# First-norm scales on TensorE, gate rows in twos, and a ScalarE copy ahead of the weights' sums in a one-layer encoder kernel

## The chip, the cores and the metric

The kernel runs on one core of a Trainium2 chip. The metric is the device time of one execution in microseconds (us); "the time" below is the median of the runs shown. The core has five engines with a queue each: TensorE (PE in the profile; its weight loads are the row PEld), VectorE (DVE), ScalarE (ACT), GpSimd (POOL) and SyncE (SP), whose queue issues the DMAs here. An engine takes its queue in order, and an instruction that waits holds up those behind it.

## The reference, cut to what matters

One transformer-like layer runs over 64 + 512 = 576 tokens of two request groups (`c_sample`, `c_prompt`), with model width 1024:

```python
mod = jax.nn.silu(c) @ w_ada + b_ada          # one row for each group
sh1, sc1, gt1, sh2, sc2, gt2 = split(mod, 6)
h = rmsnorm(x, norm1_g) * (1 + sc1) + sh1
proj = h @ w_in                               # q, k, v, GLU, two gates
m = (sigmoid(g_a) * attention @ w_attn_out + sigmoid(g_b) * conv_branch) @ w_out
x = x + gt1 * m
h2 = rmsnorm(x, norm2_g) * (1 + sc2) + sh2
gate, up = split(h2 @ w_ffn_up, 2)
x = x + gt2 * ((silu(gate) * up) @ w_ffn_down)
y = rmsnorm(x, final_g)
```

All inputs and outputs are float32.

## The kernel before, in words

The model's 1024 columns lie on the partitions as 8 tiles of 128; the 576 tokens run along the free dimension, in two halves. Every float32 weight and activation is split into a high part, rounded to the type that TensorE reads in one pass (fp32r), and a low part, the rest; a product is then three passes (`mm3`, L323 to L325). Weights come by DMA from SyncE's queue into a ring of five raw buffers (`wraw`, `load_raw`, L248). `split_unit` takes half a chunk, 128x512: ScalarE casts it to `whi` (L297), and POOL, or for some kinds VectorE, subtracts to get `wlo` (L300); each of these has four buffers. `weights` runs a few units ahead of the products.

Outside of blocks marked `manual_schedule` a planner sets the order on each engine from a simulation of times. In those blocks the order is that of the code, and the planner may put later work between.

**First norm and start of the input projection** (L501 to L582, ordered by hand). The conditioning vector is broadcast over the partitions (`cb`). For tile `k`, a scale needs a column of `w_ada`: two row products with a running sum on VectorE, one for each group (`ada_cols`, L416, tiles `dump`), called by `row`; then `scale` (L463) and `make_t` (L439) on VectorE, a high part on ScalarE (L475) and a low part on VectorE (L481), all in `make_h`. A shift is either made like that (`ROW_SH`: tiles 0 and 6) or by 8 products of 2 columns on TensorE (`ada_col`, L433), with the result in the PSUM tile `cols`. Meanwhile TensorE runs `kpass` (L498): for each tile `k` three passes (high x high, low weights x high, high weights x low of tile `k`), each over five chunks. `ada_col(k + 2)` stands ahead of the third pass of round `k`. After rounds 1 and 2, three and two split units are made.

**Up projection in pairs.** 22 pairs of a gate tile and an up tile are multiplied by a scheme of seven half-size products with sums of weights. `pair_source` makes these: for `m == 6` VectorE adds the two halves of the up chunk (L270, into a PSUM bank, `cva` or `sa` in turn) and subtracts a half of the gate chunk (L271); L274 (POOL) and L277 (VectorE) make two more sums. In `up`, VectorE's L1376, L1379, L1381, L1383 and L1387 combine product banks; ScalarE's L1373 and VectorE's L1374 make the high and low parts of the activation. Products come in three blocks of 8, 8 and 6 pairs (`FCH`), each followed by its share of the down projection (`down`, 8 output tiles, two halves each).

**Gate rows.** During the first block's down projection the last modulation (`gt2`) is made: `gate_start` loads the conditioning vectors into two `wraw` buffers and copies them into the banks `cva` and `sa`; `gate_row(n)`, once ahead of each output tile, loads one row of `w_ada` into a `wraw` buffer (L1245) and does the two row products and a bias (L1339) on VectorE.

Of the kernel before, what the change touches and what calls it, by code (L numbers as in the profile page):

```python
# [14 lines left out]
AF = mybir.ActivationFunctionType  # L15
# [4 lines left out]
P = 128  # L20
# [35 lines left out]

ROW_SH = (0, 6)

ROW_AT = 4
COL_SH = tuple(k for k in range(KT) if k not in ROW_SH)  # L60
# [27 lines left out]
def layer_kernel(ctx: ExitStack, tc: tile.TileContext, a):  # L88
# [96 lines left out]
    def vcol(o, i):  # L185
        return vec[:, o + i : o + i + 1]
# [67 lines left out]
    def pair_source(c, m):  # L254

        if m in (1, 2):
            return raws[c - 1][:, 4 * m - 4 : 4 * m]
        if m == 4:
            return raws[c][:, 4:8]
        g0, g1, u0, u1 = (raws[c - 1 + x // 2][:, 4 * (x % 2) : 4 * (x % 2) + 4] for x in range(4))  # L260
        if m == 6:

            n_sum[1] += 1
            if n_sum[1] == 1:
                sums[c, 5] = pair_sum()
                sums[c, 6] = bank("m0").rearrange("p (k n) -> p k n", n=P)
            else:
                two = bank2(("cva", "sa")[n_sum[1] % 2]).rearrange("p x (k n) -> p x k n", n=P)
                sums[c, 5], sums[c, 6] = two[:, 0], two[:, 1]
            nc.vector.tensor_add(out=sums[c, 5], in0=u0, in1=u1)  # L270
            nc.vector.tensor_sub(out=sums[c, 6], in0=sums[c, 5], in1=g0)  # L271
        elif m == 7:
            sums[c, 7] = pair_sum()
            nc.gpsimd.tensor_sub(out=sums[c, 7], in0=g0, in1=u0)  # L274
        elif m == 3:
            sums[c, 3] = pair_sum()
            nc.vector.tensor_sub(out=sums[c, 3], in0=g1, in1=sums[c, 6])  # L277
        return sums[c, m]
# [6 lines left out]

    def split_unit():
        i, key, k0, n, pair = units[state["unit"]]
# [10 lines left out]
        last = key[0] == "fd" and key[2] == len(FCH) - 1  # L298
        eng = nc.vector if last or (pair and pair[1] in LO_V) else nc.gpsimd
        eng.tensor_sub(out=lo, in0=src, in1=hi.bitcast(F32))  # L300
# [47 lines left out]
    with tc.tile_pool(name="sp", bufs=1) as sp:  # L348
# [6 lines left out]
        def load_wat(k):  # L355
# [3 lines left out]
            else:  # L359
                t = [sb([P, D], f"kv{2 * (k % 2)}"), sb([P, KT, P], f"kv{2 * (k % 2) + 1}")]  # L360
            nc.sync.dma_start(out=t[0], in_=a["w_ada_n"][k])
            if k in ROW_SH:
# [66 lines left out]
        def ada_col(k):  # L429
            if k in ROW_SH:  # L430
                return
            for i in range(KT):
                nc.tensor.matmul(  # L433
                    cols[:, 2 * k : 2 * k + 2], lhsT=wat[k][1][:, i], rhs=ct[:, i], start=i == 0, stop=i == KT - 1
                )

# [7 lines left out]
        def shift(k):  # L444
            f = SH1 + k
            src = cols[:, 2 * k : 2 * k + 2]
            if k in ROW_SH:
# [8 lines left out]
        def scale(k):  # L456
            if k == 0:
# [5 lines left out]
            nc.scalar.activation(  # L463
                out=sc_a[:, 0, k], in_=sc1[:, k], func=AF.Identity, scale=vcol(V_N1, k), bias=bsn[:, k : k + 1]
            )

        def row(k, g):
            if k < KT:
                ada_cols(sc1[:, k], wat[k][0], cbs, dumps, (g,))

        def make_h(k):
# [8 lines left out]
            for s0, s1, g in FULL:  # L480
# [3 lines left out]
                )  # L484
            if k == ROW_AT:
                for n in ROW_SH[1:]:
                    ada_cols(ada[:, SH1 + n], wat[n][1], cbs, dumps)

# [13 lines left out]
        with tc.manual_schedule(engines={ENG.PE, ENG.DVE, ENG.Activation, ENG.Pool}):  # L502
# [67 lines left out]
            for k in range(KT):  # L570
# [9 lines left out]
                for _ in range({1: 3, 2: 2}.get(k, 0)):  # L580
                    split_unit()
        nc.sync.dma_start(out=cdram.rearrange("g d -> (g d)").unsqueeze(0), in_=cb[0:1].rearrange("p g d -> p (g d)"))  # L582
# [820 lines left out]
    for c in range(len(FCH) - 1):  # L1403
# [7 lines left out]
        for n in range(8):  # L1411
            if c == 0:
                gate_row(n)
            for h in range(2):
# [175 lines left out]
```

## Time and profile before

| | |
|---|---|
| time, median of 3 runs | 952.08 us (948.9 to 953.95) |
| the profiled execution | 950.14 us, span of its instructions 948.4 us |
| mean granted clock of TensorE | 0.988 of full |
| TensorE busy | 915.4 us (97%) |
| VectorE, ScalarE, GpSimd busy | 689.8, 465.6, 530.5 us |
| DMA | 116.33 MB, mean 123 GB/s |

The profile is of one execution. Busy times of TensorE are modelled (matmuls are pipelined), an idle time is put down to whoever ended it, and the clock is given as a share of full speed, in two levels: 1.2 and 2.4 GHz.

### The profile page before, as it was taken

What the parts mean: (1) busy time and instruction counts of PE and PEld (TensorE: products, weight loads), DVE (VectorE), ACT (ScalarE), POOL (GpSimd) and SP (SyncE); (2) the same over time, 40 slices, a digit from 0 to 9 for tenths busy, and PEclk for the clock granted to TensorE, in tenths of its full rate; (3) what the DMA queues carried; (4) which work ended last, traced back from release to release, by engine and by line L of the source; (5) the groups of instructions that cost most, each with busy time, mean ns of one, the idle gap of its engine ahead of it and who ended that gap; (6) DMA issues with size and microseconds to landing.
All of it is one profiled execution on the core that took longest, in us unless ns stands there. A gap on an engine that the chain in (4) does not pass through costs nothing.

```text
span 948.4 us, 18132 instructions
## 1 busy us (share of the span) xinstructions
PE 915.4 (97%) x6804; PEld 901.8 (95%) x6804; DVE 689.8 (73%) x1372; ACT 465.6 (49%) x1055; POOL 530.5 (56%) x495
## 2 busy tenths in 40 slices
PE   7989999999999999999999999999999999999995
PEld 4989999999999999999999989999899999999995
DVE  6988999868888884589967698844566644556475
ACT  5436555466555566552434764453254541255462
POOL 2759999445454546453573565654367664376322
PEclk8999999999999999999999999999999999999997
DMA  9914423222122123286463244355322232222352
GB/s 338 360 55 53 150 77 100 68 84 68 45 68 68 46 95 106 84 305 224 180 241 112 67 134 134 112 156 198 136 90 90 89 112 72 67 96 88 88 149 100
DMA packets 37918, 116.33 MB, mean 123 GB/s; under 512 B 4243, under 2 KB 9011, under 8 KB 37685
## 3 DMA queue, kind: packets, MB, share of 16 engines
q1 hardware_dynamic: 37830, 115.18, 37.0%
q8 instruction: 53, 0.87, 0.4%
q14 instruction: 35, 0.29, 0.1%
HBM read 111.11 MB, written 4.18 MB: 122 GB/s over the span
## 4 chain that ended last, share of the span: by engine, by line
PE 66%; DVE 16%; DMA 10%; issue 4%; ACT 1%; POOL 1%; SPq 0%; DVEq 0%; ACTq 0%; POOLq 0%
PE m L323 12%; PE m L324 11%; PE m L325 11%; PE s L323 8%; PE s L325 8%; PE s L324 8%; DVE dump L416 5%; DMA wraw<-w_ada_n 3%; DMA wraw<-w_up 3%; DVE lsum L416 2%; DMA wat<-w_ada_n 2%; PE sa L923 1%; DVE h L481 1%; DVE qa L439 1%; DVE wlo L300 1%
## 5 line engine op out<-in xcount | busy, mean ns | idle before, releaser
L300 POOL TENSOR_TENSOR wlo<-wraw,whi 128x512 fp32r<-128x512 f32 x216 | 291.8, 1359 | 217.2 <-ACT whi L297 173.6
L297 ACT CAST whi<-wraw 128x512 fp32r<-128x512 f32 x248 | 149.5, 608 | 162.3 <-PE s L324 86.3
L323 PE MATMUL m<-h,whi 128*128 128x320 f32 (+2 forms) x768 | 227.0, 296 | 2.1 <-ACT whi L297 2.1
L324 PE MATMUL m<-h,whi 128*128 128x320 f32 (+2 forms) x768 | 225.8, 295 | 0.0
L325 PE MATMUL m<-h,wlo 128*128 128x256 f32 (+2 forms) x768 | 225.0, 295 | 0.2 <-DVE wlo L300 0.2
L323 PEld LDWEIGHTS m<-h,whi 128*128 128x128 f32 x768 | 145.1, 189 | 2.8 <-ACT whi L297 2.6
L325 PEld LDWEIGHTS m<-h,wlo 128*128 128x128 f32 x768 | 144.6, 189 | 0.4 <-DVE wlo L300 0.4
L324 PEld LDWEIGHTS m<-h,whi 128*128 128x128 f32 x768 | 144.8, 189 | 0.0
L671 DVE SCALAR_TENSOR_TENSOR cva<-z,vec,cva 128x606 f32<-128x606 f32 x150 | 127.5, 850 | 1.5
L323 PE MATMUL s<-h,whi 128*128 128x288 f32 (+2 forms) x336 | 99.4, 296 | 2.2 <-ACT kv L1287 1.9
L325 PE MATMUL s<-h,wlo 128*128 128x288 f32 (+2 forms) x336 | 98.9, 294 | 0.0
L324 PE MATMUL s<-h,whi 128*128 128x288 f32 (+2 forms) x336 | 98.8, 294 | 0.0
L300 POOL TENSOR_TENSOR wlo<-wx,whi 128x512 fp32r<-128x512 f32 x44 | 56.7, 1291 | 58.3 <-ACT whi L297 52.8
L324 PE MATMUL m<-qa,whi 128*128 128x288 f32 (+2 forms) x272 | 80.3, 295 | 0.0
L323 PE MATMUL m<-qa,whi 128*128 128x288 f32 (+2 forms) x272 | 80.2, 296 | 0.0
L325 PE MATMUL m<-qa,wlo 128*128 128x288 f32 (+2 forms) x272 | 79.9, 294 | 0.0
L323 PE MATMUL s<-qa,whi 128*128 128x288 f32 (+2 forms) x240 | 70.9, 296 | 0.0
L324 PE MATMUL s<-qa,whi 128*128 128x288 f32 (+2 forms) x240 | 70.9, 295 | 0.0
L325 PE MATMUL s<-qa,wlo 128*128 128x288 f32 (+2 forms) x240 | 70.4, 295 | 0.2 <-DVE wlo L300 0.2
L323 PE MATMUL s<-kv,whi 128*128 128x288 f32 x216 | 64.7, 300 | 4.5 <-DVE t L1379 3.5
L323 PEld LDWEIGHTS s<-h,whi 128*128 128x128 f32 x336 | 63.5, 189 | 2.8 <-ACT kv L1287 2.1
L324 PE MATMUL s<-kv,whi 128*128 128x288 f32 x216 | 63.9, 296 | 0.0
(421 smaller groups left out, 2332.5 us busy)
## 6 DMA issues: line engine op xcount, KB each, us to landing
wraw<-w_up SPq DMA_DIRECT2D x52, 512.0 KB, 3.3
wraw<-w_in SPq DMA_DIRECT2D x39, 512.0 KB, 3.4
wat<-w_ada_n SPq DMA_DIRECT2D x16, 512.0 KB, 3.5
wraw<-w_ada_n SPq DMA_DIRECT2D x16, 512.0 KB, 4.1
wraw<-w_dn SPq DMA_DIRECT2D x16, 512.0 KB, 3.5
wraw<-w_dn SPq DMA_DIRECT2D x16, 384.0 KB, 3.1
wraw<-w_ao SPq DMA_DIRECT2D x8, 512.0 KB, 3.4
wraw<-w_co SPq DMA_DIRECT2D x8, 512.0 KB, 4.2
```

What stands on the lines that cost most here:

```text
L297: nc.scalar.copy(out=hi, in_=src)
L300: eng.tensor_sub(out=lo, in0=src, in1=hi.bitcast(F32))
L323: nc.tensor.matmul(out, lhsT=hi, rhs=xh, start=first, stop=False, skip_group_check=again)
L324: nc.tensor.matmul(out, lhsT=hi, rhs=xl, start=False, stop=False, skip_group_check=again)
L325: nc.tensor.matmul(out, lhsT=lo, rhs=xh, start=False, stop=last, skip_group_check=again)
L416: nc.vector.scalar_tensor_tensor(out=dumps[g], in0=wt, scalar=1.0, in1=cbt[g], op0=ALU.mult, op1=ALU.mult, accum_out=out[:, g : g + 1],)
L439: nc.vector.scalar_tensor_tensor(out=xt[k][:, s0:s1], in0=xt[k][:, s0:s1], scalar=sc_a[:, 0, k, g : g + 1], in1=rstd[:, s0:s1], op0=ALU.mu ...
L481: nc.vector.scalar_tensor_tensor(out=hl[k][:, s0:s1], in0=xt[k][:, s0:s1], scalar=ada[:, f, g : g + 1], in1=hh[k][:, s0:s1].bitcast(F32), ...
L671: nc.vector.scalar_tensor_tensor(out=acc, in0=src, scalar=w, in1=acc, op0=ALU.mult, op1=ALU.add)
L923: nc.tensor.transpose(pts[0][:, j, u], probs[u][:, j].rearrange("p a b -> p (a b)"), ident)
```

## The change

Three edits stand in one diff.

1. *Sum of weights.* For every pair but the first, ScalarE copies `u0` into the PSUM bank of the sum, and the addition on VectorE then reads that bank and `u1`.
2. *Gate rows in twos.* Rows `2n` and `2n + 1` are made ahead of output tiles 0 to 3, instead of row `n` ahead of each of 8.
3. *First norm.* The five split units after rounds 1 and 2 take VectorE for the low part (`split_unit(nc.vector)`). The scales of tiles 5 and 7 (`COL_SC`) are made by products on TensorE, as is the shift of tile 6, so `ROW_SH` is tile 0 alone. `ada_col(k)` makes the scale's group and then the shift's. The columns of `w_ada` are packed accordingly on the host.

```diff
--- before.py
+++ after.py
@@ -54,9 +54,8 @@
 
 LOADS = (0, -1, 1, 2, 3, -2, 4, 5, 6, 7)
 
-ROW_SH = (0, 6)
-
-ROW_AT = 4
+ROW_SH = (0,)
+COL_SC = (5, 7)
 COL_SH = tuple(k for k in range(KT) if k not in ROW_SH)
 ENG = mybir.EngineType
 
@@ -267,7 +266,8 @@
             else:
                 two = bank2(("cva", "sa")[n_sum[1] % 2]).rearrange("p x (k n) -> p x k n", n=P)
                 sums[c, 5], sums[c, 6] = two[:, 0], two[:, 1]
-            nc.vector.tensor_add(out=sums[c, 5], in0=u0, in1=u1)
+                nc.scalar.copy(out=sums[c, 5], in_=u0)
+            nc.vector.tensor_add(out=sums[c, 5], in0=sums[c, 5] if n_sum[1] > 1 else u0, in1=u1)
             nc.vector.tensor_sub(out=sums[c, 6], in0=sums[c, 5], in1=g0)
         elif m == 7:
             sums[c, 7] = pair_sum()
@@ -283,7 +283,7 @@
         n_sum[0] += 1
         return ft([P, 4, P], f"wx{n_sum[0] % 2}")
 
-    def split_unit():
+    def split_unit(low=None):
         i, key, k0, n, pair = units[state["unit"]]
         while state["raw"] <= i:
             load_raw()
@@ -296,7 +296,7 @@
             hi, lo = where()
         nc.scalar.copy(out=hi, in_=src)
         last = key[0] == "fd" and key[2] == len(FCH) - 1
-        eng = nc.vector if last or (pair and pair[1] in LO_V) else nc.gpsimd
+        eng = low if low else nc.vector if last or (pair and pair[1] in LO_V) else nc.gpsimd
         eng.tensor_sub(out=lo, in0=src, in1=hi.bitcast(F32))
         split[key, k0] = (hi, lo)
         state["unit"] += 1
@@ -358,7 +358,11 @@
                 t = [q[:, 0], q[:, 1].rearrange("p (i n) -> p i n", n=P)]
             else:
                 t = [sb([P, D], f"kv{2 * (k % 2)}"), sb([P, KT, P], f"kv{2 * (k % 2) + 1}")]
-            nc.sync.dma_start(out=t[0], in_=a["w_ada_n"][k])
+            if k in COL_SC:
+                t[0] = t[0].rearrange("p (i n) -> p i n", n=P)
+                nc.sync.dma_start(out=t[0], in_=a["w_ada_k"][len(COL_SH) + COL_SC.index(k)])
+            else:
+                nc.sync.dma_start(out=t[0], in_=a["w_ada_n"][k])
             if k in ROW_SH:
                 t[1] = t[1].rearrange("p i n -> p (i n)")
                 nc.sync.dma_start(out=t[1], in_=a["w_ada_n"][KT + ROW_SH.index(k)])
@@ -427,12 +431,12 @@
                 )
 
         def ada_col(k):
-            if k in ROW_SH:
-                return
-            for i in range(KT):
-                nc.tensor.matmul(
-                    cols[:, 2 * k : 2 * k + 2], lhsT=wat[k][1][:, i], rhs=ct[:, i], start=i == 0, stop=i == KT - 1
-                )
+            for j, ks in enumerate((COL_SC, COL_SH)):
+                for i in range(KT if k in ks else 0):
+                    nc.tensor.matmul(
+                        cols[:, 4 * k + 2 * j : 4 * k + 2 * j + 2], lhsT=wat[k][j][:, i], rhs=ct[:, i],
+                        start=i == 0, stop=i == KT - 1,
+                    )
 
         def make_t(k):
             for s0, s1, g in FULL:
@@ -443,7 +447,7 @@
 
         def shift(k):
             f = SH1 + k
-            src = cols[:, 2 * k : 2 * k + 2]
+            src = cols[:, 4 * k + 2 : 4 * k + 4]
             if k in ROW_SH:
                 src = ada[:, f]
                 if k == 0:
@@ -461,11 +465,11 @@
                 )
                 return
             nc.scalar.activation(
-                out=sc_a[:, 0, k], in_=sc1[:, k], func=AF.Identity, scale=vcol(V_N1, k), bias=bsn[:, k : k + 1]
+                out=sc_a[:, 0, k], in_=cols[:, 4 * k : 4 * k + 2] if k in COL_SC else sc1[:, k], func=AF.Identity, scale=vcol(V_N1, k), bias=bsn[:, k : k + 1]
             )
 
         def row(k, g):
-            if k < KT:
+            if k < KT and k not in COL_SC:
                 ada_cols(sc1[:, k], wat[k][0], cbs, dumps, (g,))
 
         def make_h(k):
@@ -482,9 +486,6 @@
                     out=hl[k][:, s0:s1], in0=xt[k][:, s0:s1], scalar=ada[:, f, g : g + 1],
                     in1=hh[k][:, s0:s1].bitcast(F32), op0=ALU.add, op1=ALU.subtract,
                 )
-            if k == ROW_AT:
-                for n in ROW_SH[1:]:
-                    ada_cols(ada[:, SH1 + n], wat[n][1], cbs, dumps)
 
         def kpass(k, i):
 
@@ -578,7 +579,7 @@
                         ada_col(k + 2)
                     kpass(k, i)
                 for _ in range({1: 3, 2: 2}.get(k, 0)):
-                    split_unit()
+                    split_unit(nc.vector)
         nc.sync.dma_start(out=cdram.rearrange("g d -> (g d)").unsqueeze(0), in_=cb[0:1].rearrange("p g d -> p (g d)"))
 
     def hx(k, h):
@@ -1409,8 +1410,9 @@
             ysum = [[yt[0][:, n] for n in range(8)], [yt[1 + n // 4][:, n % 4] for n in range(8)]]
             gate_start()
         for n in range(8):
-            if c == 0:
-                gate_row(n)
+            if c == 0 and n < 4:
+                gate_row(2 * n)
+                gate_row(2 * n + 1)
             for h in range(2):
                 b = mmbank()[:, :HB]
                 down(b, n, c, h)
@@ -1520,7 +1522,8 @@
     up_order = cat([o + P * i + np.arange(P) for i in range(FT) for o in (0, DFF)])
 
     w_ada = x["w_ada"][0]
-    w_ada_k = tiles(cat([w_ada[:, P * (f + k) : P * (f + k + 1)] for k in COL_SH for f in (SH1,)], axis=1))
+    kts = [SH1 + k for k in COL_SH] + [SC1 + k for k in COL_SC]
+    w_ada_k = tiles(cat([w_ada[:, P * f : P * f + P] for f in kts], axis=1))
     fts = [SC1 + k for k in range(KT)] + [SH1 + k for k in ROW_SH]
     fts += [f + k for f in (GT1, SH2, SC2, GT2) for k in range(8)]
     w_ada_n = cont(np.stack([w_ada[:, P * f : P * f + P].T for f in fts]))
```

## Rows read from the trace of the kernel before

**Rows 1.** The page's busy table: engine, busy us, share of span, instructions.

```profile
PE 915.4 (97%) x6804; PEld 901.8 (95%) x6804; DVE 689.8 (73%) x1372; ACT 465.6 (49%) x1055; POOL 530.5 (56%) x495
```

**Rows 2.** Waits of PE, whole span: waiter, awaited, us in total, times, longest.

```profile
PE s L323 <- DVE t L1379: 3.5, 6, 0.9
...
PE m L323 <- DVE t L1379: 1.0, 1, 1.0
...
PE s L323 <- ACT qa L1373: 0.9, 1, 0.9
```

**Rows 3.** Timeline, PE, first norm: start, us, line, operation, [idle before <-releaser].

```profile
45.96 1.84 PE L433 MATMUL s<-ct,qa 128*128 128x2 f32 x16
...
47.66 0.54 PE L498 MATMUL m<-h,whi 128*128 128x320 f32 x2
...
48.95 0.46 PE L498 MATMUL m<-h,kv 128*128 128x320 f32 x2
...
50.15 0.45 PE L498 MATMUL m<-h,kv 128*128 128x320 f32 x2
...
54.94 0.56 PE L498 MATMUL m<-h,kv 128*128 128x320 f32 x2 [2.24 <-ACT h L475]
...
57.45 1.84 PE L433 MATMUL s<-ct,kv 128*128 128x2 f32 x16
...
59.40 0.56 PE L498 MATMUL m<-h,kv 128*128 128x320 f32 x2
...
71.50 0.28 PE L323 MATMUL s<-h,whi 128*128 128x256 f32 x1
```

**Rows 4.** Windows, first norm: stretch, length, busy (count) by engine, PEclk, DMA, GB/s.

```profile
45.00:47.00 2.00, 2.00 (x20) 2.00 (x18) 2.00 (x2) 0.35 (x1) 2.00 (x2) 1.00 0.91 231
...
61.00:65.00 4.00, 3.98 (x18) 3.98 (x18) 3.97 (x6) 1.13 (x4) 4.00 (x3) 0.57 0.11 46
```

**Rows 5.** Timeline, POOL (first row) and DVE, first norm.

```profile
40.85 5.19 POOL L300 TENSOR_TENSOR kv<-wraw,kv 128x512 fp32r<-128x512 f32 x3
...
41.89 3.00 DVE L481 SCALAR_TENSOR_TENSOR h<-qa,ada,h 128x64 fp32r<-128x64 f32 x2
...
50.04 0.94 DVE L481 SCALAR_TENSOR_TENSOR h<-qa,ada,h 128x64 fp32r<-128x64 f32 x2
```

**Rows 6.** DVE's groups by shape: line, operation, count, busy us, mean ns, idle before.

```profile
L300 DVE TENSOR_TENSOR wlo<-wraw,whi 128x512 fp32r<-128x512 f32 x16 | 11.4, 715 | 4.9 <-ACT whi L297 4.8
...
L271 DVE TENSOR_TENSOR sa<-sa,wraw 128x512 f32<-128x512 f32 x10 | 6.9, 686 | 0.1
```

**Rows 7.** Source view of line 172, ScalarE: durations ns min/median/max, starts.

```profile
L172 ACT COPY cva<-wraw x1: 1018/1018/1018, 630.2 to 630.2; 128x1024 f32<-128x1024 f32 x1
```

**Rows 8.** Timeline, DVE, PE and POOL, two up-projection pairs of the second block.

```profile
723.02 1.50 DVE L270 TENSOR_TENSOR cva<-wraw 128x512 f32<-128x512 f32 x1 [2.13 <-DMA wraw<-w_up]
...
725.03 0.38 PE L323 MATMUL s<-kv,whi 128*128 128x288 f32 x1 [0.34 <-DVE t L1379]
...
734.90 2.98 POOL L300 TENSOR_TENSOR wlo<-wraw,whi 128x512 fp32r<-128x512 f32 x2
...
734.97 1.78 DVE L270 TENSOR_TENSOR sa<-wraw 128x512 f32<-128x512 f32 x1 [2.40 <-DMA wraw<-w_up]
...
737.03 0.68 DVE L271 TENSOR_TENSOR sa<-sa,wraw 128x512 f32<-128x512 f32 x1
...
737.26 0.37 PE L323 MATMUL s<-kv,whi 128*128 128x288 f32 x1 [0.85 <-DVE t L1379]
```

**Rows 9.** Timeline, DVE and PE, end of the first down projection.

```profile
676.16 1.22 DVE L416 SCALAR_TENSOR_TENSOR lsum<-wraw,cva 128x1024 bf16<-128x1024 f32 x1 [2.95 <-DMA wraw<-w_ada_n]
...
678.58 0.70 DVE L270 TENSOR_TENSOR cva<-wraw 128x512 f32<-128x512 f32 x1
...
681.93 0.40 PE L323 MATMUL m<-h,whi 128*128 128x288 f32 x1 [1.72 <-ACT whi L297]
```

**Rows 10.** Windows, the same place.

```profile
682.00:686.00 4.00, 3.80 (x16) 3.57 (x17) 2.34 (x4) 2.41 (x5) 3.34 (x3) 0.57 0.06 11
```

## The prediction

> **What bounds the kernel.** I read the page's busy table first: TensorE (PE) is busy for 915.4 of 948.4 us, VectorE (DVE) for 689.8 [rows 1]. So a change to another engine is worth only what it takes away from PE's 33 us without work, or what it adds to or takes from PE's own work and clock. Then PE's waits over the span, to see who ends them, and the timeline around each wait, to see why that engine was late. Three places answer the three parts of the change.
>
> In the **first norm** PE runs the input products with hardly a gap up to 52.7 us; then it waits 2.24 us for tile 5 [rows 3], and less for tiles 6 and 7. The edit speaks of VectorE, which has no idle time here, but most of the stretch is bound by PE. Why VectorE is late: while GpSimd (POOL) splits weights from 40.85 to 46.04, two steps of VectorE that take 0.94 us elsewhere take 3.00 us [rows 5]; both engines read two SBUF tensors.
>
> In the **up-projection pairs**, the sum `u0 + u1` (L270) waits for its weights' DMA; then it takes 1.50 or, with POOL splitting beside it, 1.78 us, and 0.70 us at its shortest [rows 8, 9]. Behind it in VectorE's queue stands L1379, which frees a PSUM bank: PE then waits 0.34 or 0.85 us [rows 8]. Over the span these are 3.5 + 1.0 us in seven waits, and two waits of about 0.9 us on L1373, which follows a step that stood behind the same sum (one row stands for both) [rows 2]: 6.3 us.
>
> At the **end of the first down projection** the last gate row arrives by DMA at 676.2 us and occupies VectorE until 678.6. Both banks in which the next pairs' sums are made hold the conditioning vectors until then, so the sum starts at 678.58, and PE waits 1.72 us at 681.9 [rows 9]. Its clock then falls, to 0.57 of full in the mean of 4 us [rows 10].
>
> **First norm, part by part.** VectorE loses six row products (two groups for each of three columns): 1.22 us each, as a row product takes elsewhere [rows 9], about 1.15 net of its overlap with the next, so 6.9 us. It gains five splits of 128x512 from SBUF: 0.715 us each by the nearest group [rows 6], 3.6 us; the upper bound for one is that of a two-tensor step beside POOL, 1.8 us [rows 8]. And the two steps of 3.00 us should fall back to 0.94, 4.1 us. VectorE is so relieved by some 7 us and should no longer make PE wait. The ScalarE casts before these splits stand where they stood; three of the splits now precede `make_t(3)`, two `make_t(4)`, on VectorE, and delay tile 3 by some 1 us, behind which PE still has two rounds. POOL loses the five splits; its next work there is off the path.
>
> PE gains three groups of 8 products of 2 columns (16 passes each), 1.70 us a group (45.96 to 47.66) [rows 3]: 5.1 us on the engine that binds. From 45.96 on, PE then has five groups (one for the scale and one for the shift of tiles 5 and 7, one for the shift of tile 6), 8.5 us, and 13 passes of 1.195 us (48.95 to 50.15) [rows 3], 15.5 us: the next stage starts at 70.0, against 71.50 [rows 3]. Gain at full clock: 1.5 us. Where does the stall go? Into these groups: PE no longer waits, but works on scales.
>
> The **clock** decides whether that is left. From 61 to 65 us it was granted at 0.57 in the mean, so PE ran mostly at 1.2 GHz and lost 0.43 x 4 = 1.7 us [rows 4]. In the 4 us before PE had run one group of 2-column products (from 57.45) and then, from 59.40, half a round [rows 3]; there was no long gap. A single group between full passes kept the clock at 1.00 (45 to 47 us) [rows 4]. The change puts two groups back to back for tiles 5 and 7, 3.4 us of 2-column work each time. No row shows that, so I bound it: nothing, if such work counts, or one loss of 1.7 us behind each pair, 3.4 us. I take 3.4, because the fall at 61 us came with less 2-column work than that. First norm then: -1.5 + 3.4 = **+1.9 us**; ends -1.5 and +3.6 (a third stretch, less the rest).
>
> Here a page speaks the other way. The Trainium skill ("TensorE: Matmul & The Clock Gate", "What's actually happening") says the clock is set by how busy the engine has been recently. PE is busy for all of a group in the trace (2.00 of 2.00 us) [rows 4], so by that rule the doubled groups would leave the clock alone and the time would be the first rival's; the fall at 61 us, behind a PE that was nearly always busy, fits it badly.
>
> **Gate rows.** Each row still issues one 512 KB DMA on SyncE (SP's queue), two row products and a bias. Now two rows go ahead of each of the first four output tiles' weight loads. Rows used to come one at a time, 2.95 us of waiting and 2.4 us of products [rows 9] and a bias, some 5.7 us each; eight of them reach back from 678.6 to 633 us. With two in flight VectorE's part sets the pace at best, 8 x 2.7 behind a first landing at 636, so the last row ends between 658 us and, with half of that gained, 668. The next sums then have 14 us or more until PE needs them at 681.9. Loads of down-projection weights move behind rows in SP's queue; the ring, whose loads stand ahead of use, hides that, by how much no row shows, and a rival below prices it. If it holds, 1.7 us of waiting and the clock's loss, 0.43 x 4 = 1.7 us [rows 9, 10], go away: **-3.4 us**; if the cover is gone, 0.
>
> **Sum.** Of 22 pairs, 21 get a ScalarE copy of `u0` into the PSUM bank. A copy of twice the size took 1.018 us [rows 7]; half of that and some overhead, an estimate, is 0.6 us; bounds 0.5 and 1.0. ScalarE is half idle [rows 1]; 12.6 us in all lie beside PE. The addition then reads PSUM and SBUF, like L271, which takes 0.686 us [rows 6], whether POOL runs or not. From the landing of the DMA that makes 0.6 + 0.7 = 1.3 us and a semaphore, against 0.70 to 1.78: hardly sooner. What matters is the order on VectorE. The planner now puts the sum just ahead of L1379 and its follower L271 behind that, at 737.03 [rows 8], so in its times L1379 becomes ready within about one instruction of the sum's start. With the copy in front the addition is ready later, and L1379 should move ahead of it; then neither L1379 nor PE waits. Added wait: ScalarE's queue stands until the DMA lands; behind the copy are casts of later weight units and bank evacuations, for which PE and POOL wait. The buffers are four units deep, so a delay below about 2 us costs nothing. I take **-5.0 us** of the 6.3, leaving something for pairs where the copy comes late; ends -6.3 and +2.7 (0.45 us in each of 20 pairs, less 6.3).
>
> **Sum of the parts.** 1.9 - 3.4 - 5.0 = -6.5 us, on the profiled execution 950.14 - 6.5 = 943.6 us. That execution (span 948.4 and 1.7 around it) was 1.9 us below the median of 952.08, so on the median 945.6 us; the rivals' times stand on the median too. With PE busy 97% of the span [rows 1], what the first norm gains or loses reaches the end.
>
> **Rivals.**
> - *The clock holds* through the groups: first norm -1.5, sum -9.9, 942.2 us. For it: PE is busy by the trace, as above. Against: the fall at 61 us.
> - *The order stays*: the addition remains ahead of L1379. With 1.3 us or more from landing to its end it resembles the 1.50 us case, some 0.3 us of waiting in each of 20 pairs, 6 us, what there was. Then 1.9 - 3.4 = -1.5: 950.6 us. For it: the planner's times are not those of the chip.
> - *Rows in twos give nothing*: weights come late behind them, or the first sums wait for ScalarE. 1.9 - 5.0 = -3.1: 949.0 us.
> - *Slower: ScalarE held by the copy.* One mechanism: the planner places the copy where VectorE's sum stands, and there VectorE sat 2.1 to 2.4 us before the DMA landed [rows 8]. If ScalarE sits so long with casts behind it, a cast is 2.4 + 0.6 us late; beyond about 2 us PE waits for it, 1 us a pair, over 14 such pairs 14 us. 14 - 5.0 - 3.4 + 1.9 = +7.5: 959.6 us. It decides once the copy stands over 2 us ahead of landing with a cast behind it that is due. Against: ScalarE's casts there are paced by PE's release of buffers, mostly about when the DMA lands.
>
> **Chances.** Forecast 0.44, clock holds 0.17, order stays 0.17, rows give nothing 0.11, ScalarE held 0.11. A difference below 0.5% (4.8 us) can hardly be told from no change here; faster by more means under 947.3 us. Faster 0.61 (first two), same 0.28, slower 0.11. The range, 941 to 952 us, holds the first four cases with their bounds and leaves the last.
>
> **What would show it.** In the first norm: PE without waits for tiles 5 to 7, the next stage starting near 73.4 us, two stretches at 0.5 clock behind the doubled groups; at full clock, 70.0. At the first down projection: last gate row before 667 us, no PE wait before the first pair of the second block, clock 1.00. In the pairs: no two-SBUF L270, PE's waits on L1379 nearly gone, L1379 ahead of the addition on VectorE. The prediction is wrong if PE's waits move to ScalarE's casts, or if the planner, which sees other times everywhere, orders some distant stage worse, for which no row speaks.

## The result, and the profile after

The changed kernel takes 937.71 us (median, 936.69 to 940.77) where the kernel before, run beside it, takes 953.02: a ratio of 0.9857, 95% interval 0.9833 to 0.988, or 13.6 us. Run again later beside other kernels (last experiment) it gave 0.9885 (0.9862 to 0.9907). The prediction, 945.6 of 952.08, is a ratio of 0.993: the direction was right, the gain was about twice as large, and the time lies outside the range. The two profiled executions are 950.14 and 936.69 us, so the traces differ by 13.45 us.

PE's waits in the changed kernel, largest first (columns as in [rows 2]); line numbers have moved by one to four, L1379 is L1380 here:

```profile
PE sa L512 <- DMA kv<-crow: 5.0, 1, 5.0
PE m L157 <- ACT lsum L151: 1.6, 1, 1.6
PE sa L157 <- ACT t L151: 1.0, 1, 1.0
PE s L323 <- DVE qa L1135: 0.9, 1, 0.9
PE s L323 <- ACT kv L1288: 0.8, 1, 0.8
...
PE m L499 <- ACT h L479: 0.6, 1, 0.6
PE s L323 <- DVE t L1380: 0.2, 1, 0.2
```

Against [rows 2] the waits on the step that frees a bank have shrunk from 4.5 us in seven to 0.2 in one, those on the activation's high part are gone, and so are those on tiles 5 to 7 [rows 3] and on the first pair of the second block [rows 9]. What is left stands mostly at the start of the kernel.

**Where the 13.45 us are.** VectorE's first step of a pair (L1376 before, `u = c6 + u`) has 22 starts; the distances between them cut the second half of the run into stretches. The two traces, and those of the experiments below, in us:

| kernel | pair 1 to 8 | 8 to 9 (gate rows) | 9 to 16 | 17 to 22 |
|---|---|---|---|---|
| before | 58.61 | 65.75 | 81.96 | 57.55 |
| changed | 54.51 | 62.18 | 78.10 | 56.29 |
| sum alone | 55.21 | 65.15 | 79.83 | 56.28 |
| rows in twos alone | 58.74 | 62.59 | 83.52 | 58.58 |
| first norm alone | 58.43 | 65.57 | 81.44 | 58.59 |
| sum and rows | 55.49 | 62.18 | 78.10 | 56.28 |
| changed, order only | 57.32 | 62.18 | 78.10 | 57.04 |
| changed, copy on VectorE | 55.95 | 62.18 | 78.22 | 56.29 |

From 16 to 17 it is 61.93 us in all of them, to 0.01. So the change gains 4.10 + 3.86 + 1.26 = 9.2 us in the pairs and 3.6 at the gate rows. The first norm ends 1.94 us later than before (ScalarE's first step of the next stage at 72.63 instead of 70.69). The rest, 13.45 - 9.2 - 3.6 + 1.9 = 2.6 us, lies in between (1.7 us) and behind the last pair (0.9 us). Of that 1.1 us is one wait (at 557.06 in the trace before, on L1287) that was 1.91 us in that execution alone: it is 0.8 us in the changed kernel, but 0.8 to 1.3 us in every other trace below too, with whichever edit.

A column of pairs is read like this, here four pairs of the second block. VectorE's timeline, kernel before (start us, us, line, operation):

```profile
732.11 0.46 DVE L1376 TENSOR_TENSOR t<-m,t 128x288 f32<-128x288 f32 x1 [0.33 <-ACT t L1360]
...
744.14 0.45 DVE L1376 TENSOR_TENSOR t<-m,t 128x288 f32<-128x288 f32 x1
...
756.29 0.45 DVE L1376 TENSOR_TENSOR t<-m,t 128x288 f32<-128x288 f32 x1
...
767.42 0.45 DVE L1376 TENSOR_TENSOR t<-m,t 128x288 f32<-128x288 f32 x1
```

Pairs come every 12.03, 12.15 and 11.13 us: in this block the shortest distance is what a pair takes when nothing is late (six of the seven distances are 11.13 us in the changed kernel). In the changed kernel, VectorE again, one pair:

```profile
711.60 0.45 DVE L1377 TENSOR_TENSOR t<-m,t 128x288 f32<-128x288 f32 x1
712.96 0.46 DVE L1380 TENSOR_TENSOR t<-s,t 128x288 f32<-128x288 f32 x1 [0.91 <-PE s L325]
715.20 0.70 DVE L270 TENSOR_TENSOR cva<-cva,wraw 128x512 f32<-128x512 f32 x1 [1.78 <-ACT cva L269]
715.93 0.70 DVE L271 TENSOR_TENSOR cva<-cva,wraw 128x512 f32<-128x512 f32 x1
716.54 0.45 DVE L1382 TENSOR_TENSOR t<-s,t 128x288 f32<-128x288 f32 x1
...
722.73 0.45 DVE L1377 TENSOR_TENSOR t<-m,t 128x288 f32<-128x288 f32 x1
```

L1380 now stands ahead of the sum (L270), the sum takes 0.70 us instead of 1.50 or 1.78 [rows 8], and the next pair comes 11.13 us later. The copy on ScalarE waits for the DMA in VectorE's stead:

```profile
714.57 0.59 ACT L269 COPY cva<-wraw 128x512 f32<-128x512 f32 x1 [1.07 <-DMA wraw<-w_up]
```

**First norm.** Windows over the changed kernel (columns as in [rows 4]; the clock is the value behind the five engines):

```profile
46.00:49.50 3.50, 3.50 (x34) 3.50 (x33) 0.54 (x1) 0.00 (x0) 0.00 (x0) 1.00 0.02 8
50.00:53.30 3.30, 3.30 (x16) 3.30 (x15) 3.30 (x7) 2.79 (x7) 1.10 (x1) 0.50 0.01 2
60.00:63.00 3.00, 3.00 (x30) 3.00 (x29) 0.64 (x1) 0.59 (x2) 1.92 (x4) 1.00 0.56 179
63.70:66.90 3.20, 3.20 (x14) 3.20 (x14) 2.52 (x7) 1.50 (x4) 1.30 (x2) 0.50 0.06 11
```

The doubled groups of 2-column products start at 45.85 and 59.95 and take 3.6 us each. Behind each of them PE, busy all the time, works at 0.50 of full for 3.4 us.

**Gate rows.** VectorE, changed kernel: the end of the last row and the first sums behind it.

```profile
658.09 1.22 DVE L420 SCALAR_TENSOR_TENSOR lsum<-wraw,sa 128x1024 bf16<-128x1024 f32 x1
...
660.14 0.70 DVE L270 TENSOR_TENSOR sa<-sa,wraw 128x512 f32<-128x512 f32 x1 [0.56 <-ACT sa L269]
```

The last product ends at 659.3 instead of 678.6 [rows 9], and in the window from 676 to 680 us, in which the ninth pair starts, the clock is 1.00 and PE has no gap.

### The profile page after: what moved, and what is told of

The parts are those of the page before. It is cut to its first block, busy times and chain, and to the rows that moved or that the text cites. A ratio compares the mean times of both kernels' runs of the same rounds, so it can differ in the third digit from the quotient of the medians.

```text
span 934.9 us, 18238 instructions
## 1 busy us (share of the span) xinstructions
PE 915.1 (98%) x6852; PEld 906.1 (97%) x6852; DVE 670.1 (72%) x1365; ACT 476.7 (51%) x1076; POOL 516.3 (55%) x490
## 4 chain that ended last, share of the span: by engine, by line
PE 91%; DVE 5%; DMA 2%; ACT 1%; issue 1%; POOL 0%; SPq 0%; DVEq 0%; ACTq 0%; POOLq 0%
PE m L323 15%; PE m L325 15%; PE m L324 15%; PE s L323 11%; PE s L324 11%; PE s L325 11%; DVE dump L420 2%; PE s L436 1%; PE sa L499 1%; PE sa L924 1%; DMA qa<-xT 1%; DMA wat<-w_ada_n 1%; PE m L499 1%; PE cva L499 1%; DVE z L1080 1%; PE s L890 1%
## 5 line engine op out<-in xcount | busy, mean ns | idle before, releaser
L300 POOL TENSOR_TENSOR wlo<-wraw,whi 128x512 fp32r<-128x512 f32 x216 | 285.5, 1331 | 230.0 <-ACT whi L297 187.5
```

## The experiments

Each ratio is to the kernel before, run beside it on the same chip; us are the ratio's distance from 1 times the median of before in that comparison (949.1 to 949.7 us).

### One part at a time

The sum's edit alone, the kernel before otherwise:

```diff
-            nc.vector.tensor_add(out=sums[c, 5], in0=u0, in1=u1)
+                nc.scalar.copy(out=sums[c, 5], in_=u0)
+            nc.vector.tensor_add(out=sums[c, 5], in0=sums[c, 5] if n_sum[1] > 1 else u0, in1=u1)
```

> The kernel before with the sum of weights edit alone (copy of u0 on ScalarE, then the addition). Theory A, the sum's term was mis-sized: the three blocks of pairs in the two traces differ by -4.1, -3.9 and -1.3 us, all of it due to this edit; so about -9.2 us alone, at most -10.9 with the waits at 491 and 557 us, and nothing before 490 us. Theory B, the recorded waits are right and the rest comes from the other edits or from the planner: -5.0 to -6.3 us. In the trace by A: pairs every 11.1 us.

0.9897 (0.9875 to 0.9919): -9.8 us (-11.9 to -7.7). Theory A holds for the size; B, at most 6.3 us, lies outside. In the table's three stretches of pairs the gain is 3.4 + 2.1 + 1.3 = 6.8 us in this one trace. Between the eighth and ninth pair the gate's wait is still there (2.08 us, on the cast of the sum), and the first distance of the second block is longer for it (12.67 us, 11.30 in the changed kernel).

The gate rows in twos alone:

```diff
-            if c == 0:
-                gate_row(n)
+            if c == 0 and n < 4:
+                gate_row(2 * n)
+                gate_row(2 * n + 1)
```

> The kernel before with the gate rows in twos alone. By the prediction -3.4 us (1.7 of a wait, 1.7 of the clock); the two traces differ there by -3.6 us. Theory A: -3.5 us, last row near 659 us, no other stage moves. Theory B (the rows in twos also carry part of what the blocks of pairs gained): -5 us or more, with shorter pairs in the first or second block. Were the sum without its copy late also with the banks free early, only the clock would come back: -1.7 us.

0.9982 (0.9966 to 0.9999): -1.7 us (-3.2 to -0.1). The stretch itself gains 3.2 us, as forecast, but not all of it arrives: from pair 9 on this execution spends 2.6 us more than that of before (1.6 and 1.0). PE's waits, this kernel:

```profile
PE s L323 <- DVE t L1379: 6.1, 8, 0.8
...
PE m L323 <- DVE t L1379: 1.0, 1, 1.0
```

7.1 us in nine instead of 4.5 in seven [rows 2]. The kernel with the first norm alone also has 58.59 in the last stretch, so 1.0 of the 2.6 varies between executions where the sum is not edited; whether the rest does is open.

The first norm's edit alone, its main lines:

```diff
-ROW_SH = (0, 6)
+ROW_SH = (0,)
+COL_SC = (5, 7)
...
-                    split_unit()
+                    split_unit(nc.vector)
```

> The kernel before with the first norm's edit alone (five splits on VectorE, scales of tiles 5 and 7 and shift of tile 6 on TensorE). Theory A: +2.0 us, as the offset of the two traces behind that stage; the next stage near 73.4 us, clock at 0.5 behind both doubled groups. Theory B: the waits that went at 491 and 557 us (some 1.8 us) are this edit's, by what the planner does later: +0.2 us over the whole.

1.0006 (0.9989 to 1.0023): +0.6 us (-1.0 to +2.2). The next stage starts at 73.49 us, with the clock at 0.50 behind both doubled groups. Theory A's +2.0 is within the interval, theory B's +0.2 too. The waits at 491 and 557 us are gone or short here, but in the trace of the rows alone as well, so they didn't need this edit.

Sum and rows together, the first norm untouched; the diff is that of the first two experiments.

> The kernel before with the sum of weights and the gate rows in twos, the first norm untouched. Theory J, the parts add up: the sum alone gave -9.8 us, the rows alone -1.7: -11.5 us together, and the changed kernel's -13.6 has 2 us from the first norm. Theory K, the rows' gain of 3.5 us was given back in the next pairs where the sum was not changed, and stays where it is: -13 to -14 us, and the first norm's edit is worth -0.5 to +2 us on top.

0.9871 (0.985 to 0.9891): -12.2 us (-14.2 to -10.3). Beside the changed kernel in the same comparison, the median is 0.7 us lower (937.65 and 938.37). So all of the change's gain comes from two of its three edits, and the third gives nothing that can be told from zero. Between J and K the interval doesn't decide; the trace has the rows' 3.6 us in full (62.18) and the pairs at 78.10 and 56.28, as K says.

### What makes the sum's edit work: the order, or the short addition

Two things change for VectorE: L1380 comes ahead of the addition, and the addition takes 0.70 us. The first experiment keeps the order and takes the short addition away:

```diff
-            nc.vector.tensor_add(out=sums[c, 5], in0=sums[c, 5] if n_sum[1] > 1 else u0, in1=u1)
+            nc.vector.tensor_add(out=sums[c, 5], in0=u0, in1=u1)
```

> The changed kernel, but the addition on VectorE reads u0 and u1 from SBUF as before; the copy on ScalarE stays ahead of it (its result is overwritten), and with it the order on VectorE: L1380 ahead of the addition. Theory F, the order is what the sum's edit brought: as the changed kernel, within 1.5 us, pairs every 11.1 us, though the addition takes up to 1.8 us beside GpSimd. Theory G, the shorter addition (0.70 instead of up to 1.78 us) brought it: at least half of the 9.2 us is lost, +4.6 us or more against the changed kernel, waits on L1380 back.

0.9927 (0.9913 to 0.9942): -6.9 us, 4 to 7 us less than the changed kernel in its two comparisons, and 3.6 us less in the pairs of the trace. The table shows where: pairs 9 to 16 keep all of their gain (78.10), pairs 1 to 8 keep 1.3 of 4.1, the last 0.5 of 1.3. One of the early pairs of this kernel, first VectorE, then PE:

```profile
581.70 1.66 DVE L270 TENSOR_TENSOR sa<-wraw 128x512 f32<-128x512 f32 x1 [0.23 <-ACT sa L269]
583.27 0.45 DVE L1380 TENSOR_TENSOR t<-m,kv 128x288 f32<-128x288 f32 x1
```

```profile
582.86 0.29 PE L325 MATMUL m<-kv,wlo 128*128 128x288 f32 x1
583.87 0.37 PE L323 MATMUL m<-kv,whi 128*128 128x288 f32 x1 [0.71 <-DVE t L1380]
```

Here the addition stands ahead of L1380, and so it does in the changed kernel (VectorE):

```profile
579.02 0.70 DVE L270 TENSOR_TENSOR sa<-sa,wraw 128x512 f32<-128x512 f32 x1 [0.34 <-ACT sa L269]
579.63 0.45 DVE L1380 TENSOR_TENSOR t<-m,kv 128x288 f32<-128x288 f32 x1
```

In some early pairs the order did not move at all; there the 0.70 us is what does it. In the second block the order did move, and the length (0.85 to 1.32 us there, itself shorter than the 1.15 to 1.82 us of five of the eight before) no longer matters. F and G each hold in a block of their own.

The second experiment keeps the short addition but has VectorE make the copy, which then stands ahead of L1380:

```diff
-                nc.scalar.copy(out=sums[c, 5], in_=u0)
+                nc.vector.tensor_copy(out=sums[c, 5], in_=u0)
```

> The changed kernel with the copy of u0 made by VectorE. No step reads two SBUF tensors, but the copy, which waits for the weights' DMA, now stands on VectorE ahead of L1380. Theory F (the order): waits on L1380 come back in part, for about 0.6 us of copy stands in front instead of 1.5 to 1.8 us of addition: +3 us against the changed kernel, between +1.5 and +9. Theory G (the short addition): no waits, within 1 us of the changed kernel.

0.9906 (0.9892 to 0.9921): -8.9 us. The pairs keep 7.7 of 9.2 us; what is lost is nearly all in the first block. VectorE, second block:

```profile
716.65 0.69 DVE L269 COPY cva<-wraw 128x512 f32<-128x512 f32 x1 [2.52 <-DMA wraw<-w_up]
717.25 0.45 DVE L1380 TENSOR_TENSOR t<-s,t 128x288 f32<-128x288 f32 x1
717.62 0.69 DVE L270 TENSOR_TENSOR cva<-cva,wraw 128x512 f32<-128x512 f32 x1
```

L1380 waits behind a step that waits for the DMA, as in the kernel before [rows 8], and PE is not late, since that step takes 0.69 and not 1.5 to 1.8 us. So what counts in these two blocks is how long VectorE is held ahead of L1380: not at all or 0.7 us are both good enough. The copy on ScalarE is worth 1.6 us more in the pairs of the trace, 1.4 of it in the first block, where PE waits for L1380 twice (0.6 and 0.4 us; in the changed kernel once, 0.2). Both theories had half of it.

### What the first norm's edit costs, and why

Time from the start of the first 2-column group to ScalarE's first step of the next stage, and the stretches from that group on at which the granted clock was 0.50 (us from the span's start):

| kernel | us | at 0.50 of full |
|---|---|---|
| before | 46.1 | 61.3 to 64.7 |
| sum alone | 45.9 | 55.7 to 59.1 |
| rows alone | 45.7 | 31.3 to 34.7 |
| sum and rows | 46.9 | 60.0 to 63.4 |
| changed | 49.4 | 26.1 to 29.5, 50.0 to 53.4, 63.7 to 67.1 |
| changed, again | 49.4 | 48.9 to 55.7, 65.9 to 69.4 |
| first norm alone | 48.4 | 51.3 to 54.7, 65.0 to 68.4 |
| order only | 48.3 | 51.0 to 54.5, 64.7 to 68.1 |
| copy on VectorE | 51.1 | 26.9 to 30.3, 50.8 to 54.2, 64.4 to 67.9 |
| groups apart | 51.2 | 45.0 to 58.6 |
| 48 columns | 45.4 | none |
| splits only | 43.8 | none |
| splits only, 48 columns | 44.7 | none |
| tile 5 only, 48 columns | 42.7 | none |

The first four kernels run the same instructions there, and the clock fell once in each, at four different places; in the sum alone it fell right behind a wait of 2.32 us before tile 5, in the rows alone inside a group. In all five with the doubled groups it fell at both of them: behind the group, or, in *changed, again*, within it (the first doubled group took 4.78 us there instead of 3.63).

First I moved the scale's group two passes ahead of the shift's:

```diff
-                    if i == 2 and k + 2 < KT:
-                        ada_col(k + 2)
+                    if i != 1 and k + 2 < KT:
+                        ada_col(k + 2, (i // 2,))
...
```

> The changed kernel with the scale's group of tiles 5 and 7 ahead of the first pass of the round, two passes ahead of the shift's group, so that no two groups of 2-column products stand back to back. The work is the same. Theory C, the clock falls because two groups stand together: no stretch at 0.5 behind tiles 5 and 7, the next stage 3.4 us earlier, near 70.0 us, and the whole 3.4 us under the changed kernel. Theory D, it falls for the amount of 2-column work in the stage, however spread: still one or two falls, 0 to -1.7 us. Theory E, the clock is lost for another reason (waits at the start): no difference. If the group is early for its weights' DMA, TensorE waits there and the gain is less by that.

0.9895 (0.987 to 0.992): -10.0 us, nothing gained (-10.9 for the changed kernel in its second comparison). The move put the scale of tile 5 one pass behind the shift of tile 4:

```profile
40.80 1.84 PE L437 MATMUL s<-ct,qa 128*128 128x2 f32 x16
43.79 2.35 PE L437 MATMUL s<-ct,qa 128*128 128x2 f32 x16
50.52 3.41 PE L437 MATMUL s<-ct,qa 128*128 128x2 f32 x16
```

The clock fell in the second of these, and the third, now twice as long, came while it was down: it rose only at 58.6. Tile 7's groups, spread in the same way, brought no fall. So it is not standing back to back that does it, and theory C as I put it is out. D fits. E, which says that nothing changes, fits the time as well; the next experiment speaks against it.

Then I left the groups where they were and widened each product from 2 to 48 columns, the same two repeated:

```diff
-                        cols[:, 4 * k + 2 * j : 4 * k + 2 * j + 2], lhsT=wat[k][j][:, i], rhs=ct[:, i],
+                        cols[:, o : o + 48], lhsT=wat[k][j][:, i], rhs=ctw[:, i].rearrange("p r g -> p (r g)"),
...
```

> The changed kernel, but each 2-column product of the first norm takes 48 columns (the two of ct repeated 24 times; 47 of 48 results per pair are not read). Same count and order of products, and by the trace an 2-column product takes 0.106 us whatever it does in between. Theory C1, few columns are what precedes a fall of the clock: no stretch at 0.5 of full between 30 and 75 us except behind waits, the next stage 3.4 us earlier, near 70 us, and the time 3.4 us under the changed kernel. Theory C2, TensorE's clock doesn't depend on columns (for one, it follows how busy the engine is, and it is busy all along in both): no difference. Were a product of 48 columns longer than 0.106 us, the groups would show it.

0.9863 (0.9847 to 0.9878): -13.0 us. The groups take no longer (1.88 for 1.84 us), and PE is as busy as before; the windows of this kernel:

```profile
46.00:49.50 3.50, 3.50 (x34) 3.50 (x33) 1.10 (x3) 0.72 (x1) 0.00 (x0) 1.00 0.07 25
50.00:53.30 3.30, 3.30 (x26) 3.30 (x26) 2.77 (x5) 2.84 (x7) 1.29 (x1) 1.00 0.01 2
...
63.70:66.90 3.20, 3.20 (x26) 3.20 (x25) 1.67 (x4) 1.07 (x2) 0.85 (x2) 1.00 0.05 11
```

1.00 where the changed kernel has 0.50, and the stage is 4.0 us shorter by the table (2.9 to 5.7 against the five). With 2 columns the clock fell at 10 of 10 doubled groups, with 48 at none of the two here (and not at the one of the last kernel in the table), so C1 holds for the clock. The runs as a whole agree: their mean granted clock is 0.987 to 0.991 in 12 runs of the changed kernel and 0.990 to 0.994 in the four of this one. In the time of the whole it is not shown: 0.9863 lies between the changed kernel's two ratios, 0.9857 and 0.9885, and the 3.4 us that C1 forecast under it can't be told from nothing. The Trainium skill ("TensorE: Matmul & The Clock Gate", "What's actually happening") says that the clock follows how busy the engine has been; the trace doesn't agree if the busy time of the profile is meant, for PE is busy in all of the 3.30 us from 50.00 at either level.

### The splits without the scales

The sum, the rows in twos and the five splits on VectorE, while all scales, and the shift of tile 6, stay on VectorE. To the kernel before, beside the diffs of the sum and the rows (the argument of `split_unit` left out here):

```diff
-                    split_unit()
+                    split_unit(nc.vector)
...
```

> The kernel before with the sum of weights, the gate rows in twos, and of the first norm's edit the five splits on VectorE alone: scales of tiles 5 and 7 and the shift of tile 6 stay on VectorE. Theory H, the wait of 2.2 us before tile 5 comes from the two steps of 3.00 us beside GpSimd: without GpSimd's splits from 40.85 on they take 0.9 us, the splits cost VectorE 3.6 us and give back 4.1, the wait goes nearly away, and TensorE saves three groups of 2-column products (5.1 us) and the clock's second fall: 2 to 5 us under the changed kernel. Theory I, VectorE's load is the cause: the wait stays or grows (2 to 4 us), and the time is within 1.5 us of the changed kernel.

0.9835 (0.982 to 0.9851): -15.7 us, and 2.2 us under the kernel with 48 columns beside it. Neither theory is right as it stands. The wait before tile 5 is still there, as theory I says; the time is better, as H says. PE's wait:

```profile
54.79 0.55 PE L499 MATMUL m<-h,kv 128*128 128x320 f32 x2 [1.95 <-ACT h L476]
```

VectorE is not what makes it. Its step for tile 5 (L440, `make_t`) starts at 51.16 instead of 53.19, 2.0 us earlier than in the kernel before, nearly the 2.24 us that PE waited there. But ScalarE, which makes the high part from it, now has four casts of later weights between the two steps of that part:

```profile
51.53 0.35 ACT L476 ACTIVATE h<-qa,ada 128x64 fp32r<-128x64 f32 x1 [2.87 <-DVE qa L440]
51.93 2.18 ACT L298 CAST whi<-wraw 128x512 fp32r<-128x512 f32 x4
54.02 0.72 ACT L476 ACTIVATE h<-qa,ada 128x512 fp32r<-128x512 f32 x1
```

In the kernel before, four such casts stand behind both steps:

```profile
54.17 0.72 ACT L475 ACTIVATE h<-qa,ada 128x512 fp32r<-128x512 f32 x1 [0.25 <-DVE qa L439]
54.80 2.17 ACT L297 CAST whi<-wraw 128x512 fp32r<-128x512 f32 x4
```

So VectorE's gain was spent on ScalarE. No run moved these casts, so what the wait would be without them is not measured. The slow steps themselves: both of the prediction's steps of 3.00 us take 0.94 us now (at 42.80 and 44.86, and so in the changed kernel, at 41.99 and 44.06). A third one, tile 5's low part, took as long in the kernel before, beside later splits of GpSimd (55.55 to 58.80), and it still does, here and in the changed kernel (3.00 us at 53.06). Before, then here:

```profile
56.34 3.01 DVE L481 SCALAR_TENSOR_TENSOR h<-qa,ada,h 128x64 fp32r<-128x64 f32 x2
```

```profile
55.37 3.01 DVE L482 SCALAR_TENSOR_TENSOR h<-qa,ada,h 128x64 fp32r<-128x64 f32 x2
```

For all that the stage is 5.6 us shorter than in the changed kernel: it has three groups less (5.1 us) and no fall, and 2.9 us of waits before tiles 5 to 7.

Then the same with 48 columns, and once more with the scale of tile 5 alone on TensorE. Against the kernel with 48 columns (the second has `COL_SC = (5,)` instead):

```diff
-ROW_SH = (0,)
-COL_SC = (5, 7)
+ROW_SH = (0, 6)
+ROW_AT = 4
+COL_SC = ()
...
```

> The sum, the rows in twos and the five splits on VectorE, scales on VectorE as before, and the six shifts' products on TensorE with 48 columns instead of 2. If few columns are what precedes a fall (C1): no fall of the clock from 30 to 75 us, and 0 to 1.7 us under the same kernel with 2 columns (0.9835 of the kernel before), which showed none in its profile either, while the first norm of the kernel before fell in three of three. If not (C2): within 0.5 us of 0.9835, a fall in some place.

> As the one before, but the scale of tile 5 alone on TensorE, with 48 columns. TensorE gains one group (1.7 us) and VectorE is rid of two row products (2.3 us) ahead of tile 5; the wait before tile 5 (1.95 us) should go, and those before tiles 6 and 7 (1.0 us) with it: -1.2 us against the one before, at most; if the wait stays because tile 5 is late for another reason, +1.7 us.

Both 0.9825 (0.9802 to 0.9848 and 0.9803 to 0.9848): -16.6 us, medians 933.12 and 932.85, beside 938.37 for the changed kernel: these beat both kernels. In the last one the wait before tile 5 is gone and 0.36 us before tile 7 is all that is left; its stage is 2.0 us shorter than that of the one before, yet the medians differ by 0.3 only, which the runs can't tell apart. Whether 48 columns gain anything without the doubled groups isn't settled either: 0.9825 and 0.9835 have overlapping intervals.

The changed kernel beside these three:

> The changed kernel once more, beside the next three. Against the kernel before 0.983 to 0.988, as at first. In the first norm two falls of the clock, near 50 and 64 us, as in four of the four profiles with doubled groups so far.

0.9885 (0.9862 to 0.9907), just outside the 0.983 to 0.988 that was expected, with the two falls (the first one longer, 48.9 to 55.7).

## Why the prediction was right, and where it was wrong

**The failed step is the sum's term:** -5.0 us with a cap of 6.3 was taken, 9.2 us came in the two traces, and the edit alone measured 9.8 (7.7 to 11.9). That error, 4.2 us in the traces, is more than half of the distance between forecast and result. Two steps in it were wrong.

- *The cap.* I added up the recorded waits, 6.3 us in nine. A recorded wait is shorter than what PE loses. In the trace before, PE's starts around one of them [rows 8]:

```profile
724.40 0.29 PE L325 MATMUL s<-kv,wlo 128*128 128x288 f32 x1
725.03 0.38 PE L323 MATMUL s<-kv,whi 128*128 128x288 f32 x1 [0.34 <-DVE t L1379]
725.25 0.29 PE L324 MATMUL s<-kv,whi 128*128 128x288 f32 x1
725.38 0.29 PE L325 MATMUL s<-kv,wlo 128*128 128x288 f32 x1
```

  Starts are 0.13 us apart when nothing is late (725.25 to 725.38); here they are 0.63 and then 0.22, so 0.50 + 0.09 us are lost for 0.34 recorded. In the order-only kernel it is 0.96 lost for the 0.71 recorded above. Counted like this from PE's starts, the nine waits cost 8.4 us and not 6.3, and waits too short for the list come on top. The pitch would have shown it in one block: pairs 9 to 16 took 81.96 us, seven distances at the shortest, 11.13, make 77.9, so 4.05 us were to be had there; the change got 3.86. It is no sure way, though: in the first block, whose pairs are not alike, the shortest distance (7.25 us) would promise 7.9 us, and the change got 4.1. The range's lower end, 941 us, rested on the cap, and failed with it.

- *The mechanism.* I reckoned 0.6 + 0.7 us from the landing of the DMA, "hardly sooner" than before, so that only the order could help. But VectorE isn't held during the copy: it is held for 0.70 instead of up to 1.82 us. The order-only kernel, which has the prediction's own mechanism, keeps 5.7 us of the pairs' 9.2, near the -5.0 that was taken; the 3.6 us above that need the short addition, which the prediction put at nothing. (The two are not shares that add up: the kernel with the copy on VectorE keeps 7.7.) The rival *order stays* counted a stay as no gain; where it stayed, in the early pairs, the short addition brought the gain. That the addition needs 0.70 us whether GpSimd runs or not was forecast and is right: all 21 in the changed kernel do, and GpSimd is at work beside 16 of them. The Trainium skill ("SBUF — State Buffer", "Who interferes with whom") says that a step of VectorE with two inputs in SBUF contends with GpSimd's reads and one with a single such input doesn't. The rows agree on the second (0.70 us, 16 of 16) and mostly on the first: beside GpSimd's subtractions the additions of the kernel before took up to 1.82 us, but some took no longer than 0.71, as at 843.71.

**The gate rows** were right: -3.4 forecast, -3.6 in the changed kernel (1.7 of wait and as much of clock gone, rows over at 659 us within the forecast 658 to 668). Not forecast: alone they bring 1.7 us (0.1 to 3.2); in that trace a part is spent again in pairs that wait, and only in the traces with the sum's edit it all stays. I added terms that are not quite independent.

**The first norm** was right in every step that the prediction lists: no wait of PE before tiles 5 to 7, two stretches at 0.5, +1.9 forecast and +1.94 in the trace, and the rival *clock holds* is out. From 45.96 to PE's first product of the next stage at 71.50 it counted right, for the changed kernel takes 2.1 us more (45.85 to 73.45). That the offset to the whole trace comes out alike is in part luck: the first group started 1.4 us earlier there, and a third fall at 26.1, which was not forecast, took about as much back. And the ground for taking two falls, the one at 61 us, was weak, since with the same instructions it comes at another place in each of four traces. Measured on the whole it is +0.6 (-1.0 to +2.2). By the stage's own length it costs 1.4 to 2.7 us where there was no third fall and the two were short (48.3 and 48.4 against 45.7 to 46.9), for the clock falls in the kernel before as well, but once. Its premise on the two steps of 3.00 us was right: both fell to 0.94.

**ScalarE held by the copy** didn't occur: in the trace of the changed kernel most copies wait 0.1 to 1.2 us (3.0 and 4.8 us at the gate rows), not 2.4, and PE waits for no cast behind them.

**The rest:** 2.6 us outside these stretches had no row. 1.1 of it was an unusually long wait in the profiled execution of the kernel before; for the other 1.5 no single cause was found; 0.9 of it lies behind the last pair, where the traces differ by as much among themselves (60.6 to 61.5 us).

## What to carry to other kernels

Don't size what a repeated unit can gain by adding up recorded waits: nine of them made 6.3 us here and cost 8.4. Where the units are alike, their distance from their own shortest pitch is better (4.05 us for a measured 3.86); where they are not, it promises too much (7.9 for 4.1). When a step is taken off an engine's queue, ask how long that engine is held ahead of the work that is due, not when the step's result comes. And cut a bundle of edits apart before keeping it: one of the three here brought nothing that can be told from zero, and the kernels without its larger half came to 0.9825 to 0.9835, against 0.9871 without any of it and 0.9857 and 0.9885 with all of it.

## What the runs showed of the hardware

- The granted clock fell to 0.50 while PE was busy without a gap, behind or within both doubled groups of 2-column products in five of five traces, and at none of the three doubled groups with products 48 columns wide, which take 1.88 us a group for 1.84. Widening these products cost TensorE next to nothing here; that it makes the whole kernel faster is not shown.
- With the same instructions the fall comes at different places from one execution to the next (31, 56, 60 and 61 us): one profile shows that a fall occurs, not where.
- A group that started while the clock was down took 3.41 instead of 1.84 us, and that fall was the longest of all, 45.0 to 58.6 us (one trace; that the group prolonged it is not shown by itself).
